# Short branch: both duals' first products ahead, weight sums on VectorE, loads on GpSimd's queue, and T4 later in the FFN front

## The chip, the core and the metric

The kernel runs on one core of one Trainium2 chip. The engines are named as the profile names them: PE is TensorE, DVE VectorE, ACT ScalarE, Pool GpSimd, and SP SyncE, which only issues transfers here. The metric is the device time of one execution in microseconds (us).

## The reference

One layer of a streaming encoder, in fp32, with 1024 positions and a width of 1024. A combined projection of the normalized input feeds two mixers and their gates; their merge goes through one more projection, and a gated FFN follows.

```python
h = rms_norm(x, norm_mix_g[l]) * (1.0 + sc1) + sh1
proj = jnp.einsum('bsd,de->bse', h, w_in[l])
b_s, c_s, v_s, v_c, gl_c, gate_br = jnp.split(proj, SPLITS[:-1], axis=-1)
y_a = b_s * causal_dwconv(c_s * v_s, conv_short_w[l])          # the short branch
y_a = jnp.einsum('bsc,cd->bsd', y_a, w_short_out[l])
u = v_c * jax.nn.sigmoid(gl_c)                                 # the conformer branch
u = causal_dwconv(u, conv_conf_w[l]) + conv_conf_b[l]
u = jax.nn.silu(layer_norm(u, conf_ln_g[l], conf_ln_b[l]))
y_b = jnp.einsum('bsc,cd->bsd', u, w_conf_out[l])
g_a, g_b = jnp.split(jax.nn.sigmoid(gate_br), 2, axis=-1)
x = x + g1 * jnp.einsum('bsd,de->bse', g_a * y_a + g_b * y_b, w_o[l])
h2 = rms_norm(x, norm_ffn_g[l]) * (1.0 + sc2) + sh2
a, bgate = jnp.split(jnp.einsum('bsd,df->bsf', h2, w_ffn_in[l]), 2, axis=-1)
x = x + g2 * jnp.einsum('bsf,fd->bsd', jax.nn.silu(a) * bgate, w_ffn_out[l])
return rms_norm(x, final_norm_g)
```

## The kernel before, in words

**Products.** Every fp32 operand is split in a high part (a cast to fp32r on ACT, `...h`) and a low part (source minus high part, on DVE or Pool, `...l`). `mm3` multiplies with three matmuls: high by high (L291), low activation by high weight (L292), high activation by low weight (L294). For weights the cast is L209 (`wh`) and the low part L210 (`wl`).

**Duals.** A pair of weight column blocks with their 1024 columns is one "dual": a 2x2 product of blocks done with seven products instead of eight, called "1", "2", "6", "5", "7", "3", "4" in this order (`PRODUCTS`). `dual_units` makes the weight operand of each. Unit "6" needs three sums of weight blocks (L233, L234, L235), unit "3" one (L237); units "1", "2" and "4" need none. `eng` says which engine sums, and by default also makes the low parts; `lo` overrides that per unit. With `early=True` each unit loads its own blocks when it is made. On the activation side the operands need differences too, such as T3 and T4 in the FFN (B22 is a plain block). The results gather in pairs of PSUM banks x, y and z; a product's result that starts a sum in another bank is copied there by ACT.

**Order.** `plan` lists the weight operands in the order of use. `next_w` takes one and lets `fetch` make those after it, so that about three are under way. Raw blocks land in `raws`, five tiles used in turn, loaded through SP's queue. The instructions of each engine are put in order by the framework's list scheduler; `tc.issue_after(ins)` makes an instruction wait its turn behind another.

**The stages that matter.** After eleven input duals come:
- the short branch, "ya": two duals, 14 products (`ya_order`, `ya_product`), on operands `tq` that `q_operands` builds. Its results are multiplied by gates `ma` that come back from HBM (`gate_dram`; L554, L557). Beside it runs the LayerNorm of the conformer branch: `ln_mean` (a matmul with ones, L732), `ln_square` per channel block, with a load of `cv`, a subtraction L743, a square and a sum L749, and `ln_rstd` (a matmul, L755).
- "yb", the conformer projection, then the join of both branches, the output projection and the second norm;
- the FFN input, 11 duals, of which the first three (`FRONT`) are interleaved with the norm: `norm_2_first`, `norm_2_half` and `norm_2_last` build the operands ("t1" for product 5, "t3" for 7, "b22" for 3, "t4" for 4). Products run in `in_order`: ... (0,"6"), (0,"5"), (0,"7"), (0,"3"), (0,"4"), (1,"6"), and so on. `in_evac` empties the banks: products 1, 6 and 5 by a copy on ACT (L980), the others by sums on DVE (L985, L989, L990) and a silu.
- hidden activations go to HBM through Pool's queue, and the FFN output follows.

Of the kernel before, what the change touches and what calls it, by code (L numbers as in the profile page):

```python
# [111 lines left out]
def block_kernel(ctx: ExitStack, tc: tile.TileContext, x0, xT, c, vecs, ada, w_first, w_plain, w_duals,  # L112
# [38 lines left out]
    def s_tile(name, dt=F32):  # L151
        return hl_tile(name, dt)
# [35 lines left out]
    def raw_tile(n=1024):  # L188

        raws.append(raws.pop(0))  # L190
        return raws[-1].tile([P, 1024], F32, tag="raw", name="raw")[:, :n]

    def load(src, n=1024):
# [21 lines left out]
    def dual_units(mats, n, early=False, eng=nc.vector, lo=None):  # L215

        a = {}

        def get(*blocks):
            for b in blocks:  # L220
                a[b] = load(mats[("11", "12", "21", "22").index(b)], n)

        def unit(m):
            if early:
                get(*{"1": ("11",), "2": ("12",), "6": ("21", "22", "11"), "3": ("12",), "4": ("22",)}.get(m, ()))
            elif m == "1":
                get("11", "12", "21", "22")
            los = (lo or {}).get(m, eng)
            if m in "12":
                return split_w(a["1" + m], n, (), los)  # L230
            if m == "6":
                a["s1"] = a["22"] if early else raw_tile(n)
                eng.tensor_tensor(a["s1"], a["21"], a["22"], ALU.add)  # L233
                eng.tensor_tensor(a["21"], a["21"], a["11"], ALU.add)  # L234
                eng.tensor_tensor(a["11"], a["11"], a["s1"], ALU.add)  # L235
            elif m == "3":
                eng.tensor_tensor(a["12"], a["12"], a["11"], ALU.add)  # L237
            return split_w(a[{"6": "11", "5": "s1", "7": "21", "3": "12", "4": "22"}[m]], n, (), los)

        return {m: (lambda m=m: unit(m)) for m in PRODUCTS}  # L240
# [4 lines left out]
    for d in range(len(PAIRS) // 2):  # L245
        units = dual_units([w_duals[d, m] for m in range(4)], 1024, eng=nc.gpsimd)
        plan += [units[m] for m in PRODUCTS]
    ya_order = [(d, m) for d in range(2) for m in "12"] + [(d, m) for d in range(2) for m in PRODUCTS[2:]]
    ya_units = [dual_units([w_short[d, m] for m in range(4)], 1024, True, nc.gpsimd, {m: nc.vector for m in "65734"})
                for d in range(2)]  # L250
    plan += [ya_units[d][m] for d, m in ya_order]
    plan += [(w[k], 1024) for w in (w_conf, w_o) for _ in range(2) for k in range(KC)]
# [76 lines left out]
    def t_split(src, hi, lo):  # L329
        nc.scalar.copy(hi, src)  # L330
        t_split.ins = nc.vector.tensor_tensor(lo, src, f32(hi), ALU.subtract).ins  # L331

    def minus(out, a, b):

        nc.vector.scalar_tensor_tensor(out=out, in0=a, scalar=-1.0, in1=b, op0=ALU.mult, op1=ALU.subtract)
# [83 lines left out]
    def uc_tile(name, n=T + CK - 1, dt=F32):  # L419
        return ucp.tile([P, T + CK - 1], dt, tag="uc", name=name)[:, :n]  # L420
# [153 lines left out]
    def q_operands(m):  # L574

        for k in range(KH):
            b11, b12, b21, b22 = (q_block(k, i) for i in range(4))
            if m == "6":
                nc.vector.tensor_tensor(b11, b11, b12, ALU.subtract)
                t2 = g_tile("t2")  # L580
                minus(t2, b11, b22)
                tq[m][k] = split(t2, hl_tile, "tq")
                minus(b21, t2, b21)
                continue
            if m == "7":
                nc.vector.tensor_tensor(b12, b22, b12, ALU.subtract)
            tq[m][k] = split({"1": b11, "2": b21, "5": b11, "7": b12, "3": b22, "4": b21}[m], hl_tile, "tq")
# [148 lines left out]

    sqs = [None, None]

    def ln_square(j):
        cv.append(uc_tile(f"cv{j}", T))  # L740
        nc.sync.dma_start(cv[j], cv_dram[j])
        for h in range(2):
            nc.vector.tensor_tensor(cv[j][:, halves[h]], cv[j][:, halves[h]], mu[h], ALU.subtract)  # L743
            sq = g_tile("sq")
            nc.scalar.activation(sq, cv[j][:, halves[h]], AF.Square, scale=1.0 / 32.0)
            if j == 0:
                sqs[h] = sq
            else:
                nc.vector.tensor_tensor(sqs[h], sqs[h], sq, ALU.add)  # L749
# [34 lines left out]
    for j in range(KC):  # L784
        conv(j)
        add_conv(j)
    ma = {}
    r0, r1, r2 = banks
    ya_banks = [{"x": r0, "y": r1, "z": r1}, {"x": r2, "y": r1, "z": r0}]
    ya_rest = {}  # L790

    def ya_product(d, m):

        w = next_w()
        bank = ya_banks[d][{"2": "y", "5": "z", "3": "z"}.get(m, "x")]
        ga = {}
        if m in "2734":
            for p in range(2):
                j, h = 2 * (2 * d + p) + (m in "74"), int(m in "73")
                ma[j, h] = ga[p] = s_tile(f"ma{j}{h}")  # L800
                nc.sync.dma_start(ga[p], gate_dram["a", j][:, halves[h]])
        for p in range(2):
            ps = bank[p]
            for k in range(KH):
                c0 = (p * KH + k) * P
                mm3([ps], slice(c0, c0 + P), w, [tq[m][k]], m in "15" and k == 0, k == KH - 1, m not in "15")
            if m == "1":
                nc.scalar.copy(ya_banks[d]["y"][p], ps)
            elif m in "65":
                ya_rest[p, m] = s_tile("v")  # L810
                nc.scalar.copy(ya_rest[p, m], ps)
            elif m == "2":
                ma["ins"] = times(ga[p], ps, ga[p]).ins
            elif m == "7":
                v = ya_rest[p, "5"]
                nc.vector.tensor_tensor(v, ps, v, ALU.add)
                ma["ins"] = minus_times(ga[p], v, ga[p]).ins
            elif m == "3":
                nc.vector.tensor_tensor(ps, ps, ya_rest[p, "6"], ALU.add)
                ma["ins"] = times(ga[p], ps, ga[p]).ins  # L820
            else:
                ma["ins"] = minus_times(ga[p], ps, ga[p]).ins

    for i, (d, m) in enumerate(ya_order):
        with ExitStack() as order:
            if i == 0:
                order.enter_context(tc.issue_after(mm3.ins))
            ya_product(d, m)
        if i in (0, 3):
            q_operands("34"[i == 3])  # L830
        elif i == 2:
            mu = ln_mean()
        elif 5 <= i < 10:
            for j in range(*((0, 2), (2, 4), (4, 6), (6, 7), (7, 8))[i - 5]):
                ln_square(j)
        elif i == 10:
            rl = ln_rstd(sqs)
        elif i == 12:
            act_b(0, 0)


    mg = [[None, None] for _ in range(KC)]

    def join(o, h, g):
# [75 lines left out]
    def norm_2_last():  # L920

        for k in range(KH):
            ts["5"][k] = t_pair("t1")
            t_split(x1[k][:, halves[0]], *ts["5"][k])
        for k in range(KH):
            b12, b22 = x1[k][:, halves[1]], x1[k + KH][:, halves[1]]
            nc.vector.tensor_tensor(b12, b22, b12, ALU.subtract)
            ts["7"][k] = t_pair("t3")
            t_split(b12, *ts["7"][k])
        for k in range(KH):  # L930
            ts["3"][k] = t_pair("b22")
            t_split(x1[k + KH][:, halves[1]], *ts["3"][k])
        b21 = [x1[k + KH][:, halves[0]] for k in range(KH)]
        for k in range(KH):
            minus(b21[k], t2[k], b21[k])
        for k in range(KH):
            ts["4"][k] = t_pair("t4")
            t_split(b21[k], *ts["4"][k])
        norm_2_last.ins = t_split.ins

    sums = {}
    for h in range(2):
# [15 lines left out]
    def in_unit(d, m):  # L958

        if d in range(1, FRONT) and m == "6":  # L960
            with tc.issue_after(norm_2_last.ins):
                return in_units[d][m]()
        return in_units[d][m]()

# [96 lines left out]
    for d, m in in_order[2 * FRONT - 1 :]:  # L1061
        if (d, m) == (FRONT - 1, "2"):
            for p in range(2):
                in_evac(d)(p, "1", in_banks[d]["x", p])
        if d in range(1, FRONT) and m == "6":
            with tc.issue_after(mm3.ins):
                in_product(d, m)
        else:
            in_product(d, m)
        if m == PRODUCTS[-1]:  # L1070
            if 2 <= d < 6:
                for i in range(40 + 2 * (d - 2), 42 + 2 * (d - 2)):
                    modulation(i, x1ap.tile([P, T], F32, tag="x1", name="ada"))
            hid_set(d)
# [211 lines left out]
```

## Time and profile before

| | us |
|---|---|
| median of 3 runs (lowest to highest) | 1493.35 (1493.24 to 1495.61) |
| the profiled execution's own time | 1494.31 |
| its span, first to last instruction | 1492.5 |
| mean granted TensorE clock | 0.996 |

| engine | busy us |
|---|---|
| PE | 1458.9 |
| DVE | 1186.0 |
| ACT | 643.6 |
| Pool | 554.4 |

A timeline row reads: start, duration, engine, line, operation, output <- input, shape, count, and in brackets the idle time ahead of it and what ended that. Rows ending in q (SPq) are an engine's queue issuing transfers. Instructions are named by line and tile; of the two versions the later one's lines are some two to twenty higher.

### The profile page before, as it was taken

Reading aid. Unit: us, or ns where it says so; the run is one execution under the profiler, and the core shown is the slowest. Engines: PE = TensorE matmul, PEld = TensorE weight load, DVE = VectorE, ACT = ScalarE, POOL = GpSimd, SP = SyncE. Lnnn points to the kernel's source line nnn. Section 1 sums busy time; section 2 is a strip of 40 time slices with the busy share of each in tenths; the row PEclk is TensorE's granted clock in tenths of the full one; section 3 lists DMA queues with packets and bytes.
Section 4 is the critical chain, followed back from the end, with each engine's and each line's share of the span. In section 5 each row is a group of like instructions: output and inputs, shape, how many; then the busy total and the mean of one; then the engine's idle time right before and its main releaser. Section 6 shows DMA issues by size and latency. Waiting matters only on the chain.

```text
span 1492.5 us, 17732 instructions
## 1 busy us (share of the span) xinstructions
PE 1458.9 (98%) x6407; PEld 1192.0 (80%) x6407; DVE 1186.0 (79%) x1615; ACT 643.6 (43%) x926; POOL 554.4 (37%) x455
## 2 busy tenths in 40 slices
PE   6999999999999998999999999999999999999997
PEld 2788888888888886778888878888888888888887
DVE  7994999989999976989687698876766665677755
ACT  4663434444433354555345464444444443222235
POOL 0027777776877676500021001100000016544005
PEclk9999999999999999999999999999999999999999
DMA  9622223223222345565585348654444449998403
GB/s 344 225 71 99 99 86 113 99 99 132 94 71 71 106 134 179 191 223 190 163 271 198 123 127 259 227 180 148 147 149 148 154 151 372 355 302 264 148 15 114
DMA packets 85882, 247.78 MB, mean 166 GB/s; under 512 B 9761, under 2 KB 11937, under 8 KB 85794
## 3 DMA queue, kind: packets, MB, share of 16 engines
q1 hardware_dynamic: 44224, 142.63, 29.0%
q0 software_dynamic: 35664, 91.24, 18.6%
q10 hardware_dynamic: 5906, 12.78, 2.2%
q8 instruction: 50, 0.82, 0.2%
q14 instruction: 38, 0.31, 0.1%
HBM read 186.31 MB, written 60.29 MB: 165 GB/s over the span
## 4 chain that ended last, share of the span: by engine, by line
PE 39%; issue 15%; POOL 3%; DVE 3%; DMA 2%; ACT 0%; POOLq 0%; DVEq 0%; ACTq 0%; SPq 0%
PE x L291 7%; PE x L292 7%; PE x L294 7%; PE z L292 3%; PE z L291 3%; PE z L294 3%; PE y L294 2%; PE y L292 2%; PE y L291 2%; DMA hid<-stage 1%; DVE cv L743 1%; DMA raw<-in_w_short 1%; PE yb L292 1%; PE yb L294 1%; PE yb L291 1%
## 5 line engine op out<-in xcount | busy, mean ns | idle before, releaser
L209 ACT CAST wh<-raw 128x1024 fp32r<-128x1024 f32 (+2 forms) x263 | 265.6, 1011 | 454.0 <-PE z L292 129.3
L210 DVE TENSOR_TENSOR wl<-raw,wh 128x1024 fp32r<-128x1024 f32 (+2 forms) x175 | 201.3, 1151 | 83.6 <-ACT wh L209 81.5
L210 POOL TENSOR_TENSOR wl<-raw,wh 128x1024 fp32r<-128x1024 f32 x88 | 219.9, 2502 | 108.4 <-ACT wh L209 108.4
L701 DVE SCALAR_TENSOR_TENSOR c<-diff,vec,c 128x512 f32<-128x512 f32 x248 | 176.5, 749 | 2.2
L1005 POOL DMA_DIRECT2D hid<-stage x71 | 37.8, 533 | 356.6 <-DVE stage L331 353.4
L292 PE MATMUL x<-tl,wh 128*128 128x512 f32 x240 | 93.4, 389 | 0.0
L294 PE MATMUL x<-th,wl 128*128 128x512 f32 x240 | 93.4, 389 | 0.0
L291 PE MATMUL x<-th,wh 128*128 128x512 f32 x240 | 93.4, 389 | 0.0
L233 POOL TENSOR_TENSOR raw<-raw 128x1024 f32<-128x1024 f32 x14 | 42.7, 3053 | 116.9 <-DVE wl L210 94.9
L701 DVE SCALAR_TENSOR_TENSOR c<-u,wsum,c 128x512 f32<-128x512 f32 x112 | 83.9, 749 | 2.0 <-ACT c L705 0.4
L291 PE MATMUL z<-th,wh 128*128 128x512 f32 x168 | 65.4, 389 | 0.0
L292 PE MATMUL z<-tl,wh 128*128 128x512 f32 x168 | 65.4, 389 | 0.0
L294 PE MATMUL z<-th,wl 128*128 128x512 f32 x168 | 65.4, 389 | 0.0
L330 ACT CAST stage<-g 128x512 fp32r<-128x512 f32 x62 | 38.3, 621 | 52.8 <-DMA hid<-stage 25.5
L331 DVE TENSOR_TENSOR stage<-g,stage 128x512 fp32r<-128x512 f32 x62 | 42.4, 686 | 19.9 <-ACT stage L330 19.8
L1031 POOL DMA_DIRECT2D th<-hid x71 | 38.1, 536 | 52.3 <-PE x L294 31.2
L272 DVE CUSTOM_DVE_ANT_0 ada<-ada,cs,vec 128x1024 f32<-128x1024 f32 x33 | 48.5, 1486 | 7.9 <-DMA ada<-in_ada 7.9
L294 PEld LDWEIGHTS x<-th,wl 128*128 128x128 f32 x240 | 45.1, 188 | 9.4
L292 PEld LDWEIGHTS x<-tl,wh 128*128 128x128 f32 x240 | 45.1, 188 | 9.3
L291 PEld LDWEIGHTS x<-th,wh 128*128 128x128 f32 x240 | 45.1, 188 | 9.3
L292 PE MATMUL y<-tl,wh 128*128 128x512 f32 x132 | 51.3, 389 | 0.0
L291 PE MATMUL y<-th,wh 128*128 128x512 f32 x132 | 51.3, 389 | 0.0
(921 smaller groups left out, 4281.7 us busy)
## 6 DMA issues: line engine op xcount, KB each, us to landing
hid<-stage POOLq DMA_DIRECT2D x71, 512.0 KB, 4.5
raw<-in_w_fi SPq DMA_DIRECT2D x53, 512.0 KB, 4.2
raw<-in_w_duals SPq DMA_DIRECT2D x48, 512.0 KB, 3.5
th<-hid POOLq DMA_DIRECT2D x71, 256.0 KB, 5.7
tl<-hid POOLq DMA_DIRECT2D x71, 256.0 KB, 5.7
ada<-in_ada SPq DMA_DIRECT2D x33, 512.0 KB, 6.2
raw<-in_w_fo SPq DMA_DIRECT2D x24, 384.0 KB, 5.8
raw<-in_w_conf SPq DMA_DIRECT2D x16, 512.0 KB, 4.2
```

Of the source, the lines that this page charges most:

```text
L209: nc.scalar.copy(wh, raw)
L210: lo = lo_engine.tensor_tensor(wl, raw, f32(wh), ALU.subtract)
L233: eng.tensor_tensor(a["s1"], a["21"], a["22"], ALU.add)
L272: nc.vector.tensor_tensor_reduce(out=raw, in0=raw, in1=cs, scale=1.0, scalar=col(V_ADA, b), op0=ALU.mult, op1=ALU.add, accum_out=modc(b),)
L291: nc.tensor.matmul(ps, wh, xh, start=first, stop=False, skip_group_check=again)
L292: nc.tensor.matmul(ps, wh, xl, start=False, stop=False, skip_group_check=again)
L294: mm3.ins = nc.tensor.matmul(ps, wl, xh, start=False, stop=last, skip_group_check=again).ins
L330: nc.scalar.copy(hi, src)
L331: t_split.ins = nc.vector.tensor_tensor(lo, src, f32(hi), ALU.subtract).ins
L701: tap.ins = nc.vector.scalar_tensor_tensor(out=out, in0=src[:, s : s + H], scalar=wt, in1=acc, op0=ALU.mult, op1=ALU.add).ins
L1005: nc.gpsimd.dma_start(hid_dram[key], s)
L1031: nc.gpsimd.dma_start(t, hid_dram[key][:, s])
```

## The change

In the short branch:
- `ya_order` runs product 1 of both duals, then product 2 of both, then the rest. Dual 1's "y" gets two banks of its own from the ps2 pool; before, both duals used `r1`.
- The eight weight sums go from Pool to DVE. Of the low parts of products 1 and 2, only that of (0,"1") stays on Pool; three more go to DVE.
- The eight loads of `cv` and the sixteen of gates go from SP's queue to Pool's. The `cv` loads are issued at the start, the gates one product ahead (`ya_gate`).
- The mean comes before the first product, the squares after products 2 to 8 (counted from 0) instead of 5 to 9, and their subtraction is ordered behind the last split; `q_operands("4")` follows product 1 instead of 3, the first `act_b` product 11 instead of 12.
- The tile `diff`, free after the convolution, is a sixth raw buffer.

In the FFN front T4's four differences and splits leave `norm_2_last` for `norm_2_t4`, emitted just before product (0,"7") and ordered behind B22's splits. Unit (0,"4") is ordered behind B22's splits, and the "6" units of duals 1 and 2 behind T4's.

```diff
     def raw_tile(n=1024):
         raws.append(raws.pop(0))
+        if raws[-1] is diffp:
+            return diffp.tile([P, T + CK - 1], F32, tag="diff", name="raw")[:, :n]
...
-    ya_order = [(d, m) for d in range(2) for m in "12"] + [(d, m) for d in range(2) for m in PRODUCTS[2:]]
-    ya_units = [dual_units([w_short[d, m] for m in range(4)], 1024, True, nc.gpsimd, {m: nc.vector for m in "65734"})
+    ya_order = [(d, m) for m in "12" for d in range(2)] + [(d, m) for d in range(2) for m in PRODUCTS[2:]]
+    ya_units = [dual_units([w_short[d, m] for m in range(4)], 1024, True, lo={"1": nc.vector if d else nc.gpsimd})
                 for d in range(2)]
...
+    def cv_load(j):
+        cv.append(uc_tile(f"cv{j}", T))
+        nc.gpsimd.dma_start(cv[j], cv_dram[j])
     def ln_square(j):
-        cv.append(uc_tile(f"cv{j}", T))
-        nc.sync.dma_start(cv[j], cv_dram[j])
         for h in range(2):
-            nc.vector.tensor_tensor(cv[j][:, halves[h]], cv[j][:, halves[h]], mu[h], ALU.subtract)
+            with tc.issue_after(split.ins):
+                nc.vector.tensor_tensor(cv[j][:, halves[h]], cv[j][:, halves[h]], mu[h], ALU.subtract)
...
+    raws.insert(0, diffp)
+    mu = ln_mean()
-    ya_banks = [{"x": r0, "y": r1, "z": r1}, {"x": r2, "y": r1, "z": r0}]
+    ya_banks = [{"x": r0, "y": r1, "z": r1}, {"x": r2, "y": [ps2_tile("y") for _ in range(2)], "z": r0}]
+    def ya_gate(d, m):
+        for p in range(2):
+            j, h = 2 * (2 * d + p) + (m in "74"), int(m in "73")
+            ma[j, h] = ya_gates[d, m, p] = s_tile(f"ma{j}{h}")
+            nc.gpsimd.dma_start(ma[j, h], gate_dram["a", j][:, halves[h]])
     def ya_product(d, m):
-        ga = {}
-        if m in "2734":
-            for p in range(2):
...
-                nc.sync.dma_start(ga[p], gate_dram["a", j][:, halves[h]])
+        ga = [ya_gates.get((d, m, p)) for p in range(2)]
...
     for i, (d, m) in enumerate(ya_order):
+        if i == 0:
+            for j in range(KC):
+                cv_load(j)
+        for e in ya_order[i + 1 : i + 2]:
+            if e[1] in "2734":
+                ya_gate(*e)
...
-        if i in (0, 3):
-            q_operands("34"[i == 3])
-        elif i == 2:
-            mu = ln_mean()
-        elif 5 <= i < 10:
-            for j in range(*((0, 2), (2, 4), (4, 6), (6, 7), (7, 8))[i - 5]):
+        if i in (0, 1):
+            q_operands("34"[i])
+        elif 2 <= i < 9:
+            for j in range(*((0, 2), (2, 3), (3, 4), (4, 5), (5, 6), (6, 7), (7, 8))[i - 2]):
                 ln_square(j)
         elif i == 10:
             rl = ln_rstd(sqs)
-        elif i == 12:
+        elif i == 11:
             act_b(0, 0)
+    raws.remove(diffp)
...
+        norm_2_last.b22 = t_split.ins
+    def norm_2_t4():
         b21 = [x1[k + KH][:, halves[0]] for k in range(KH)]
         for k in range(KH):
-            minus(b21[k], t2[k], b21[k])
+            with tc.issue_after(t_split.ins):
+                minus(b21[k], t2[k], b21[k])
...
-        norm_2_last.ins = t_split.ins
+        norm_2_t4.ins = t_split.ins
     def in_unit(d, m):
         if d in range(1, FRONT) and m == "6":
-            with tc.issue_after(norm_2_last.ins):
+            with tc.issue_after(norm_2_t4.ins):
                 return in_units[d][m]()
+        if (d, m) == (0, "4"):
+            with tc.issue_after(norm_2_last.b22):
+                return in_units[d][m]()
...
+        if (d, m) == (0, "7"):
+            norm_2_t4()
```

What that does to the engines' order shows at three places. First Pool's queue at the start of the short branch, before and then after; `wl` and `raw` are the weights' low parts and blocks, the last of the six `wl` in a row is that of (0,"1").

```order
L210 TENSOR_TENSOR wl<-raw,wh 128x1024 x6
L233 TENSOR_TENSOR raw<-raw 128x1024
L210 TENSOR_TENSOR wl<-raw,wh 128x1024
L234 TENSOR_TENSOR raw<-raw 128x1024
L210 TENSOR_TENSOR wl<-raw,wh 128x1024
L235 TENSOR_TENSOR raw<-raw 128x1024
L210 TENSOR_TENSOR wl<-raw,wh 128x1024
L237 TENSOR_TENSOR raw<-raw 128x1024
```

```order
L212 TENSOR_TENSOR wl<-raw,wh 128x1024 x6
L743 DMA cv_4481<-cv_967 128x1024
L743 DMA cv_4483<-cv_968 128x1024
L743 DMA cv_4485<-cv_969 128x1024
L743 DMA cv_4487<-cv_970 128x1024
L805 DMA ma_4545<-gate_a_107 128x512
L805 DMA ma_4547<-gate_a_109 128x512
L743 DMA cv_4489<-cv_971 128x1024
```

Pool's arithmetic ends with the `wl` of (0,"1"); what follows is loads, dual 0's first gates fifth and sixth.

Second, DVE around its first multiplications by gates (L557, then L559); `tq` are the activation operands, `y` the bank that product 2 fills. With their numbers the rows before are:

```order
L323 TENSOR_TENSOR tql_4518<-sc7_3426,tqh_4517 128x512
L210 TENSOR_TENSOR wl_4567<-raw_4561,wh_4566 128x1024
L557 TENSOR_TENSOR ma00_4527<-y_981,ma00_4527 128x512
L557 TENSOR_TENSOR ma20_4529<-y_982,ma20_4529 128x512
L323 TENSOR_TENSOR tql_4637<-sc4_2697,tqh_4636 128x512
```

and after, where wl_4552 is of (1,"2"), wl_4611 of (0,"6") and wl_4655 of (0,"5"):

```order
L239 TENSOR_TENSOR raw_4736<-raw_4736,raw_4605 128x1024
L212 TENSOR_TENSOR wl_4500<-raw_4497,wh_4499 128x1024
...
L212 TENSOR_TENSOR wl_4552<-raw_4549,wh_4551 128x1024
...
L212 TENSOR_TENSOR wl_4611<-raw_4605,wh_4610 128x1024
L325 TENSOR_TENSOR tql_4590<-sc6_3419,tqh_4589 128x512
L325 TENSOR_TENSOR tql_4594<-sc7_3426,tqh_4593 128x512
L559 TENSOR_TENSOR ma00_4545<-y_981,ma00_4545 128x512
L748 TENSOR_TENSOR cv0_4481<-cv0_4481,tot0_975 128x512
L748 TENSOR_TENSOR cv0_4481<-cv0_4481,tot1_976 128x512
L748 TENSOR_TENSOR cv1_4483<-cv1_4483,tot0_975 128x512
L559 TENSOR_TENSOR ma20_4547<-y_982,ma20_4547 128x512
L748 TENSOR_TENSOR cv1_4483<-cv1_4483,tot1_976 128x512
L212 TENSOR_TENSOR wl_4655<-raw_4603,wh_4654 128x1024
```

The sum L239 and the low parts stand on DVE ahead of the multiplications, and the squares' subtractions between them and the next low part.

Third, ACT in the FFN front, before and then after; the L980 (then L1003) copies empty bank z of product (0,"5").

```order
L330 CAST t3h<-x_6016 128x512
L209 CAST wh<-raw 128x1024
L330 CAST b22h<-x_6057 128x512
L209 CAST wh<-raw 128x1024
L330 CAST b22h<-x_6098 128x512
L330 CAST b22h<-x_6139 128x512
L330 CAST b22h<-x_6180 128x512
L330 CAST t4h<-x_6057 128x512
L330 CAST t4h<-x_6098 128x512
L330 CAST t4h<-x_6139 128x512
L330 CAST t4h<-x_6180 128x512
L980 COPY g_6915<-z 128x512
```

```order
L332 CAST t3h<-x_5936 128x512
L211 CAST wh<-raw 128x1024
L332 CAST t3h<-x_5977 128x512
L332 CAST t3h<-x_6018 128x512
L332 CAST b22h<-x_6059 128x512
L332 CAST b22h<-x_6100 128x512
L332 CAST b22h<-x_6141 128x512
L332 CAST b22h<-x_6182 128x512
L1003 COPY g_6897<-z 128x512
L1003 COPY g_6912<-z 128x512
L332 CAST t4h<-x_6059 128x512
L332 CAST t4h<-x_6100 128x512
```

The copies stand ahead of T4's casts. On DVE the sums of (1,"6") follow T4's splits in both; after the change two of bank z's operations stand among them:

```order
L331 TENSOR_TENSOR t4l<-x_6180,t4h 128x512
L985 TENSOR_TENSOR g_6915<-x,g_6915 128x512
L985 TENSOR_TENSOR g_6930<-x,g_6930 128x512
L233 TENSOR_TENSOR raw<-raw 128x1024
L234 TENSOR_TENSOR raw<-raw 128x1024
L272 ISA ada,mod<-ada,cs,vec 128x1024
L272 ISA mod 128x1
L235 TENSOR_TENSOR raw<-raw 128x1024
```

```order
L1008 TENSOR_TENSOR g_6912<-x,g_6912 128x512
L333 TENSOR_TENSOR t4l<-x_6182,t4h 128x512
L235 TENSOR_TENSOR raw<-raw 128x1024
L1012 TENSOR_TENSOR g_6861<-z,g_6861 128x512
L236 TENSOR_TENSOR raw<-raw 128x1024
L1013 TENSOR_TENSOR g_6861<-g_6861,g_6897 128x512
L237 TENSOR_TENSOR raw<-raw 128x1024
```

The last sum (L235, then L237) has moved behind L1012 and L1013, and the adaLN reduction L272 has left its place.

More of the change, by code (lines that the diff above doesn't have):

```diff
@@ L786, in block_kernel @@
         add_conv(j)
+    raws.insert(0, diffp)
     ma = {}
     r0, r1, r2 = banks
-    ya_banks = [{"x": r0, "y": r1, "z": r1}, {"x": r2, "y": r1, "z": r0}]
+    mu = ln_mean()
+    ya_banks = [{"x": r0, "y": r1, "z": r1}, {"x": r2, "y": [ps2_tile("y") for _ in range(2)], "z": r0}]
     ya_rest = {}
+    ya_gates = {}
+    def ya_gate(d, m):
[3 more added lines that the diff above has]
+            nc.gpsimd.dma_start(ma[j, h], gate_dram["a", j][:, halves[h]])
     def ya_product(d, m):
@@ L795, in ya_product @@
         bank = ya_banks[d][{"2": "y", "5": "z", "3": "z"}.get(m, "x")]
-        ga = {}
-        if m in "2734":
-            for p in range(2):
-                j, h = 2 * (2 * d + p) + (m in "74"), int(m in "73")
-                ma[j, h] = ga[p] = s_tile(f"ma{j}{h}")
-                nc.sync.dma_start(ga[p], gate_dram["a", j][:, halves[h]])
+        ga = [ya_gates.get((d, m, p)) for p in range(2)]
         for p in range(2):
```

## The prediction

> **What bounds the kernel now.** I read the page's busy shares first, then the windows to find where TensorE (PE) is not full, then PE's waits in those stretches, and then the timelines of the engines that it waits for.
>
> ```profile
> PE 1458.9 (98%) x6407; PEld 1192.0 (80%) x6407; DVE 1186.0 (79%) x1615; ACT 643.6 (43%) x926; POOL 554.4 (37%) x455
> 550.00:600.00 50.00, 44.96 (x184) 34.93 (x183) 37.37 (x43) 25.46 (x42) 28.39 (x10) 0.97 0.50 173
> 600.00:650.00 50.00, 47.47 (x203) 37.59 (x203) 46.05 (x57) 24.93 (x37) 19.98 (x6) 1.00 0.56 193
> 850.00:900.00 50.00, 46.76 (x198) 37.65 (x197) 49.97 (x72) 31.39 (x48) 0.00 (x0) 0.97 0.37 116
> ```
>
> PE is the bound: 98% of the span. So the change can only bring what PE loses at present. The windows (length, then busy time of PE, weight load, DVE, ACT, Pool, then PE's clock) show three stretches where PE is short of 50 us; the first two are the short branch, the third the front of the FFN. In the third DVE is full (49.97), in the first it is not (37.37). PE's waits from 560 to 670 (the three longest) and from 860 to 925, as total, times and longest, are:
>
> ```profile
> PE z L294 <- POOL wl L210: 3.0, 1, 3.0
> PE y L291 <- ACT y L808: 1.7, 1, 1.7
> PE x L291 <- DVE v L816: 1.3, 1, 1.3
> ...
> PE z L291 <- ACT g L980: 3.2, 1, 3.2
> PE z L294 <- DVE wl L210: 0.6, 1, 0.6
> ```
>
> **Part A, the short branch: what PE loses.** Five rows of PE's timeline give the size (start, duration): the first matmul of product 1 and the first of product 2 of dual 0, the mean, the variance, and the first matmul of the next stage, yb.
>
> ```profile
> 571.15 0.39 PE L291 MATMUL x<-tqh,wh 128*128 128x512 f32 x1
> 576.59 0.49 PE L291 MATMUL y<-tqh,wh 128*128 128x512 f32 x1
> 593.15 1.88 PE L732 MATMUL mu<-tot,ones 128*128 128x512 f32 x4
> 644.09 1.88 PE L755 MATMUL var<-sq,ones 128*128 128x512 f32 x4
> 662.17 0.39 PE L291 MATMUL yb<-zsh,wh 128*128 128x512 f32 x1
> ```
>
> A product of 24 matmuls takes 576.59 - 571.15 = 5.44 us. Fourteen products and the two sums over partitions need 14 x 5.44 + 2 x 1.88 = 79.9. The stage takes 662.17 - 571.15 = 91.0. PE loses 11.1 us, which bounds the gain of part A from above.
>
> Where it goes is one chain:
>
> ```profile
> 583.05 0.39 PE L292 MATMUL z<-tql,wh 128*128 128x512 f32 x1
> 586.40 0.57 PE L294 MATMUL z<-tqh,wl 128*128 128x512 f32 x1 [2.97 <-POOL wl L210]
> 590.39 0.40 PE L291 MATMUL z<-tqh,wh 128*128 128x512 f32 x1
> 596.72 0.50 PE L291 MATMUL y<-tqh,wh 128*128 128x512 f32 x1 [1.68 <-ACT y L808]
> 563.33 4.81 POOL L210 TENSOR_TENSOR wl<-raw,wh 128x1024 fp32r<-128x1024 f32 x1 [4.62 <-ACT wh L209]
> ...
> 581.63 2.42 POOL L234 TENSOR_TENSOR raw<-raw 128x1024 f32<-128x1024 f32 x1 [3.99 <-DMA raw<-in_w_short]
> 586.37 5.01 SPq L195 DMA_DIRECT2D raw<-in_w_short  x2
> 591.48 1.80 SPq L801 DMA_DIRECT2D ma<-gate_a  x4
> 595.31 1.41 DVE L557 TENSOR_TENSOR ma<-y,ma 128x512 f32<-128x512 f32 x2 [3.20 <-DMA ma<-gate_a]
> 596.09 0.57 ACT L808 COPY y<-z 128x512 f32<-128x512 f32 x1 [5.81 <-DVE ma L557]
> ```
>
> Pool's sum L234 stands ahead of the low part (wl) of dual 1's product 1, and waits 3.99 us for a block; so PE waits 2.97 us for that wl. The ten matmuls after it take 590.39 - 586.40 = 3.99 us where ten at the usual spacing, 5.44 / 24 = 0.227, take 2.27: a slow clock of 0.97 in that window, 1.7 us more. Meanwhile SP holds the gate loads behind two weight loads that wait for Pool's wl; the gates are issued at 591.48, DVE multiplies at 595.31, and only then may ACT copy dual 1's start (its product 1 stands in the banks that the profile calls z) into bank y, which both duals share. That is PE's second wait. The waits after 620 have another cause:
>
> ```profile
> 599.22 1.23 DVE L210 TENSOR_TENSOR wl<-raw,wh 128x1024 fp32r<-128x1024 f32 x1
> 611.20 10.54 POOL L233 TENSOR_TENSOR raw<-raw 128x1024 f32<-128x1024 f32 x1 [16.87 <-DVE sq L749]
> 573.09 6.31 DVE L323 TENSOR_TENSOR tql<-q,tqh 128x512 fp32r<-128x512 f32 x4 [1.33 <-ACT tqh L322]
> 579.32 2.49 DVE L323 TENSOR_TENSOR tql<-sc,tqh 128x512 fp32r<-128x512 f32 x4
> 589.79 2.32 DVE L210 TENSOR_TENSOR wl<-raw,wh 128x1024 fp32r<-128x1024 f32 x1 [7.98 <-ACT wh L209]
> 622.22 2.88 DVE L554 SCALAR_TENSOR_TENSOR ma<-v,ma 128x512 f32<-128x512 f32 x1
> ```
>
> Beside Pool's sums, DVE and Pool slow each other: four tql splits take 6.31 us beside Pool and 2.49 alone, one wl 2.32 against 1.23, a product L554 2.88, and a Pool sum 10.54 where L234 above takes 2.42.
>
> **What the change takes and adds there.** Dual 1's banks of its own remove the wait of ACT for DVE's multiply. The sums and three low parts leave Pool, so the 3.99 us block on Pool and the slow pairs go. They are added to DVE: 8 sums and 3 wl, 11 x 1.23 = 13.5 us, of which successive ones overlap a little. DVE has that: its idle time in the chain was 1.33 + 7.98 + 3.20 = 12.5 us, and the slow rows just quoted alone give back (6.31 - 2.49) + (2.32 - 1.23) = 4.9, with more in the second set of sums. What DVE has in front of PE decides: PE's n-th product would start at 571.15 + 1.88 + 5.44 x (n - 1). Adding up the rows' durations along DVE's new order (an estimate), the wl of the second product is done at about 572 against PE's 579, that of (0,"6"), the fifth, at 587 against 595, of (0,"5") at 593 against 600, of (1,"6"), the tenth, at 616 against 622. It stays 6 to 8 us ahead, so I take the whole 11.1, with half of it as the lower bound.
>
> The loads move to Pool's queue. They are 24 issues (8 of cv, 16 of gates), and Pool has one row of arithmetic left in this stage. The nearest issue from Pool is that of the gates for branch b:
>
> ```profile
> L856 POOL DMA_DIRECT2D gb<-gate_b x16: 536/536/722, 645.4 to 746.2; - x16
> ```
>
> Each takes 0.54 us of Pool at the median, 0.72 at most, among DVE work. 24 x 0.54 = 13 us over 80 us, and six issues before dual 0's first gate are 3.2 us: hidden. SP loses the same 24 issues, so its weight loads no longer stand behind cv and gates. The diff tile as a sixth raw buffer only lets loads start sooner. The mean ahead of the first product and squares sooner move work; they cost PE the same 1.88 us each. The extra issue_after on the subtractions holds DVE's squares behind the split; what is behind them in DVE's queue is the next wl, which has the 6 to 8 us.
>
> **Part B, the FFN front.** PE reaches product 3 of dual 0 at 882.71, one spacing after 882.48:
>
> ```profile
> 882.48 0.39 PE L294 MATMUL x<-t3h,wl 128*128 128x512 f32 x1
> 886.11 0.50 PE L291 MATMUL z<-b22h,wh 128*128 128x512 f32 x1 [3.24 <-ACT g L980]
> 893.33 0.39 PE L291 MATMUL x<-t4h,wh 128*128 128x512 f32 x1
> 879.41 1.05 ACT L209 CAST wh<-raw 128x1024 fp32r<-128x1024 f32 x1 [3.77 <-DVE raw L237]
> 883.40 2.17 ACT L330 CAST t4h<-x 128x512 fp32r<-128x512 f32 x4
> 885.48 1.05 ACT L980 COPY g<-z 128x512 f32<-128x512 f32 x2
> 892.39 1.22 DVE L235 TENSOR_TENSOR raw<-raw 128x1024 f32<-128x1024 f32 x1
> 893.52 0.68 DVE L989 TENSOR_TENSOR g<-z,g 128x512 f32<-128x512 f32 x1
> 893.70 2.00 ACT L209 CAST wh<-raw 128x1024 fp32r<-128x1024 f32 x2 [4.16 <-DVE raw L235]
> ```
>
> The copies that free bank z (885.48) stand behind four t4h casts on ACT (2.17), and those behind wh, which waited 3.77 us for a sum of DVE. So product 4 starts at 893.33 instead of 882.71 + 5.44 = 888.15: 5.2 us lost, its slow clock included (again 0.97). In the new order the copies stand ahead of t4h and T4's four differences leave DVE's queue in front of that sum (4 x 0.6 = 2.4 us, as t4l's spacing, 2.49 for four in the tql row of the same shape). ACT's copies end at about 882.5, so the 5.2 us go.
>
> What is late next: T4's differences and splits now stand on DVE ahead of the sums of (1,"6"), with the second wait as before: L235 ended 893.6, and the new order puts two more half-width operations (1.2 us) in front of the last sum and moves one adaLN reduction of about that size behind it. I put the last sum's end at 893.6 to 894.8, its wh 1 us later. PE, no longer held, wants (1,"6") at 888.15 + 5.44 = 893.6, and waits 2.1 us for the high part and 0.4 for the low. The later wait of 0.6 for a wl loses about 0.5 of itself. Part B is 5.2 - 2.5 + 0.5 = 3.2; bounds 0 (the new wait eats all) and 5.7.
>
> The new wait's clock is one place for a rule. In this trace a wait of 1.68 us was not followed by slow matmuls, waits of 2.97 and 3.24 were. A wait of 2.1 lies nearer to the first, so I take no slow clock; the other end is 1.7 us more. [...]
>
> **The sum.** 11.1 + 3.2 = 14.3 us. The profiled execution took 1494.31 (span 1492.5), the median of three runs is 1493.35; the gain is taken from the profiled spans, so 1493.35 - 14.3 = 1479.0, and 1480.0 for an execution like the profiled one. About 0.2%, 3.0 us, is what a measurement here can tell from no change.
>
> **Rivals.**
> 1. *The new wait eats part B.* DVE is full in 850 to 900, so anything added ahead of (1,"6")'s sums is paid one for one. With a wait of 3 us and 1.7 of slow clock part B falls to about 0.5, 1482. For: 49.97 of 50 busy. Against: the work ahead of the last sum hardly grows. Chance 0.15.
> 2. *No new wait in the FFN.* If the sums come in time, 5.7 instead of 3.2: 1476.5. Chance 0.10.
> 3. *DVE becomes the bound of the short branch.* 13.5 us are added to a stage in which DVE was busy 46.05 of 50 us from 600 to 650. If half of part A returns as waits for wl, the time is 1484.6. For: the second window. Against: the slow pairs there (2.88 for 0.68) are Pool's doing and go with its sums. Chance 0.18.
> 4. *The gain is given back later*, where PE waits for nothing now but DVE is busy too (yb and join): 1490 to 1493. Chance 0.04.
> 5. *Slower: Pool's queue as the bound.* Pool issues in order, and dual 0's first gates stand fifth and sixth. DVE multiplies by them ahead of the wl of (0,"5"), so late gates stop PE. If an issue beside DVE's work took as long as the sum at 611.20 was stretched, 10.54 - 2.42 = 8 us, six issues from 568 (the end of Pool's wl of 563.33, which stays) would end at 616, land some 5 us later, and with 3 us more to that wl PE, which wants it at 600, would wait 24 us: 1479.0 + 24 = 1503. It turns to a loss from about 6.4 us an issue ((14.3 + 600 - 568 - 8) / 6). Against it: 0.54 in the row of gb. Chance 0.08. [...]
>
> **Chances and range.** The forecast holds 0.45, with its own range of 1477.5 to 1481.5. Cases 1 to 3 and the forecast together are 0.88 and all faster; case 4 is the no change, 0.04; case 5 slower, 0.08. The range of 8 in 10 runs from case 2 less 1.5 of term errors, 1475.0, to just over case 3, 1486.0.
>
> **What would show it.** PE's first matmul of yb should come 79 to 81 us after the mean's start; its waits for POOL wl, ACT y and DVE v should be gone, and no Pool arithmetic of 10 us be left. DVE's 128x512 operations should read 0.68 throughout the stage. In the FFN, ACT g ahead of product 3 should be gone, and a wait of about 2 us for ACT wh stand at (1,"6") in its place. A stage over 86 us with waits for DVE wl would be rival 3; long idle of DVE ahead of L559 for ma would be rival 5.

## The result and the profile after

| | us |
|---|---|
| before, median of 5 runs (lowest to highest) | 1493.25 (1493.04 to 1495.61) |
| after, median of 5 runs | 1482.34 (1480.81 to 1487.19) |
| ratio after / before, 95% interval | 0.9929, 0.9909 to 0.9949 |
| the profiled execution after, and its span | 1482.34, 1480.6 |

The change makes the kernel 0.7% faster, 10.9 us by the medians. The forecast was 1479.0 with a range of 1475.0 to 1486.0; the time lies inside that range, but outside the forecast's own band of 1477.5 to 1481.5. After's runs spread over 6 us, before's over 2.6.

The same rows as before, from the page and the windows (length, then busy PE, weight load, DVE, ACT, Pool, then PE's clock, the DMA engines' share and GB/s):

```profile
PE 1454.6 (98%) x6407; PEld 1189.3 (80%) x6407; DVE 1184.1 (80%) x1626; ACT 641.8 (43%) x926; POOL 528.1 (36%) x468
550.00:600.00 50.00, 50.00 (x219) 40.70 (x218) 44.77 (x56) 28.99 (x48) 17.38 (x21) 1.00 0.61 223
600.00:650.00 50.00, 48.99 (x211) 39.02 (x210) 45.31 (x64) 24.02 (x34) 5.34 (x10) 1.00 0.54 182
850.00:900.00 50.00, 48.26 (x210) 38.63 (x209) 47.33 (x67) 30.63 (x47) 2.13 (x5) 1.00 0.43 136
```

From 550 to 600 PE is full (44.96 before) and its clock is 1.00 where it was 0.97. From 850 to 900 PE is busy 48.26 (46.76 before), and its clock is 1.00 there too. PE's waits from 560 to 670, then from 850 to 920:

```profile
PE yb L294 <- DVE zsl L325: 1.2, 1, 1.2
PE z L293 <- DVE v L826: 0.7, 1, 0.7
PE x L293 <- DVE v L826: 0.3, 1, 0.3
...
PE x L293 <- ACT wh L211: 1.7, 1, 1.7
```

The waits for Pool's low part and for ACT's y are gone. Of the waits for DVE's v 0.3 and 0.7 are left, and two new waits stand there, one in yb (1.2) and one in the FFN front (1.7). The stage's ends, then the second's start in the FFN front, from PE's timeline:

```profile
570.77 1.88 PE L734 MATMUL mu<-tot,ones 128*128 128x512 f32 x4
652.20 0.39 PE L293 MATMUL yb<-zsh,wh 128*128 128x512 f32 x1
653.77 0.50 PE L294 MATMUL yb<-zsl,wh 128*128 128x512 f32 x1 [1.18 <-DVE zsl L325]
874.89 0.39 PE L293 MATMUL z<-b22h,wh 128*128 128x512 f32 x1
887.66 0.50 PE L293 MATMUL x<-t2h,wh 128*128 128x512 f32 x1 [1.68 <-ACT wh L211]
```

The stage took 652.20 - 570.77 = 81.4 us, 9.6 less than before's 91.0. Following the two traces' starts of the same matmuls, the gain is 10.0 us at yb (0.4 stood before the stage began), 8.4 at the mix, 7.8 before product (0,"3"), 12.2 once the front is over, and 11.9 at the end (the spans: 1492.5 - 1480.6).

Where part A fell short shows on DVE. Its waits from 570 to 655 after, and the landing times of the `cv` loads and of the gates (lowest, median, highest):

```profile
DVE ma L559 <- DMA ma<-gate_a: 5.0, 2, 3.0
DVE raw L274 <- DMA raw<-in_ada: 4.7, 1, 4.7
DVE raw L239 <- DMA raw<-in_w_short: 0.2, 1, 0.2
...
DMA to landing us min/median/max: 5.4/9.0/9.9
...
DMA to landing us min/median/max: 2.9/7.2/10.1
```

Before, `cv` landed in 5.5 us and the gates in 5.0 (medians). Pool's queue shows when the loads are asked for:

```profile
580.04 2.31 POOL L743 DMA_DIRECT2D cv<-cv  x4 [14.62 <-DVE tql L325]
582.34 1.07 POOL L805 DMA_DIRECT2D ma<-gate_a  x2
```

The first `cv` load waits 14.6 us, until DVE's splits have read the tile that it is to fill, and dual 0's first gates stand behind four `cv` loads. From there eight loads of 512 KB and the first gates are asked for within ten microseconds; from 580 to 600 the DMA engines are busy 0.99 of the time (0.69 before), and the first two gates land 9.2 and 9.6 us after they were asked for. DVE stands still 5.0 us for gates, with the wl of (0,"5") behind it, and later 4.7 for an adaLN block that stands in its order ahead of the variance's reciprocal root. That used up most of the 6 to 8 us that DVE was ahead. The low part of (1,"6"), and PE's first use of it:

```profile
620.28 1.22 DVE L212 TENSOR_TENSOR wl<-raw,wh 128x1024 fp32r<-128x1024 f32 x1
622.54 0.39 PE L296 MATMUL z<-tqh,wl 128*128 128x512 f32 x1
```

It is done at 621.5, where the estimate was 616; 1 us was left.

### The profile page after: what moved, and what is told of

It is laid out like the page before. It is cut to its first block, busy times and chain, and to the rows that moved or that the text cites. A ratio compares the mean times of both kernels' runs of the same rounds, so it can differ in the third digit from the quotient of the medians.

```text
span 1480.6 us, 17737 instructions
## 1 busy us (share of the span) xinstructions
PE 1454.6 (98%) x6407; PEld 1189.3 (80%) x6407; DVE 1184.1 (80%) x1626; ACT 641.8 (43%) x926; POOL 528.1 (36%) x468
## 4 chain that ended last, share of the span: by engine, by line
PE 86%; DVE 6%; issue 3%; DMA 2%; POOL 2%; ACT 0%; POOLq 0%; ACTq 0%; DVEq 0%
PE x L293 10%; PE x L294 10%; PE x L296 10%; PE z L294 7%; PE z L296 7%; PE z L293 7%; PE y L296 6%; PE y L294 6%; PE y L293 6%; PE yb L294 2%; PE mix L293 2%; PE yb L296 2%; PE mix L294 2%; PE mix L296 2%; PE yb L293 2%
## 5 line engine op out<-in xcount | busy, mean ns | idle before, releaser
L212 POOL TENSOR_TENSOR wl<-raw,wh 128x1024 fp32r<-128x1024 f32 x85 | 209.7, 2471 | 108.4 <-ACT wh L211 108.4
L212 DVE TENSOR_TENSOR wl<-raw,wh 128x1024 fp32r<-128x1024 f32 (+2 forms) x178 | 204.4, 1149 | 49.5 <-ACT wh L211 47.9
L235 POOL TENSOR_TENSOR raw<-raw 128x1024 f32<-128x1024 f32 x12 | 29.8, 2483 | 95.3 <-DVE wl L212 94.5
```

The costliest lines, as they stand in the source:

```text
L212: lo = lo_engine.tensor_tensor(wl, raw, f32(wh), ALU.subtract)
```

## The experiments

Each kernel ran beside the kernel before on the same chip; times are medians.

| kernel | us | before beside it | difference |
|---|---|---|---|
| after, second time | 1482.93 | 1493.66 | -10.7 |
| short branch alone | 1483.61 | 1493.28 | -9.7 |
| FFN alone | 1490.25 | 1493.28 | -3.0 |
| sums and low parts on DVE, alone | 1488.17 | 1493.04 | -4.9 |
| order, banks, mean first, alone | 1497.47 | 1493.66 | +3.8 |
| after, sums back on Pool | 1498.67 | 1493.28 | +5.4 |
| after, sums on Pool and loads on SP | 1498.64 | 1493.66 | +5.0 |
| after, no diff tile | 1485.49 | 1493.04 | -7.6 |
| after, cv loads spread | 1479.76 | 1493.66 | -13.9 |
| after, loads on SP | 1480.11 | 1493.28 | -13.2 |
| loads on SP, sums first in the FFN | 1479.66 | 1493.04 | -13.4 |
| the same, cv loads spread | 1478.97 | 1493.04 | -14.1 |

**Each part alone.** The first keeps all but the FFN's edits, the second has only those. Of the first's edit, the last lines:

```diff
...
-        if (d, m) == (0, "7"):
-            norm_2_t4()
...
```

> The short branch's edits without the FFN's. In the trace of the changed kernel the gain over the kernel before stands at 10.0 us when yb starts (0.4 of it from before the short branch), at 8.4 when the mix starts and at 7.8 in the FFN front. My theory: the two parts are independent, so this kernel keeps 8 us: 1485, with PE's wait of about 3.2 us for ACT's copies of g in the FFN front as before, its slow clock included. Rival: an FFN front that is reached earlier finds its operands no readier, or a later stage gives the gain back; then the time is above 1489. Rival: nearly all comes from here and the FFN edit only moves a wait: below 1483.

> The kernel before with only the FFN's edits (T4 behind B22). My theory: 4 to 4.5 us, 1489, as the gain grew from 7.8 to 12.2 us over the FFN front in the changed kernel's trace; a wait of about 1.7 us for ACT wh at (1,"6") without slow matmuls. Rival: the wait there is longer than 2.97 us or brings the slow clock, and the part gives under 2 us: above 1491.

1483.61 (ratio 0.9939, 0.9926 to 0.9951) and 1490.25 (0.9979, 0.9970 to 0.9988). They add up to 12.7 against 10.7 to 10.9 together, within their spread; the FFN alone brought less than the 4 to 4.5 I expected. In the first, PE waits for nothing in the stage and 0.6 us for zsl. Its stage takes 650.52 - 570.84 = 79.7 us, 1.7 less than in the profile of after, though the code of the short branch is the same. Its clock is 0.97 again from 850 to 900, with the old wait:

```profile
PE z L293 <- ACT g L995: 3.2, 1, 3.2
```

In the second that wait is gone, the clock there is 1.00, and PE waits 1.7 us for ACT's wh at (1,"6"), as in after.

**The sums back on Pool, with the loads on Pool or on SP.**

```diff
-    ... dual_units([w_short[d, m] for m in range(4)], 1024, True, lo={"1": nc.vector if d else nc.gpsimd})
+    ... dual_units([w_short[d, m] for m in range(4)], 1024, True, nc.gpsimd, {m: nc.vector for m in "65734"})
```

> The changed kernel with the eight weight sums and the three low parts back on Pool. My theory: Pool's in-order sums are the cause of most of part A; PE waits for POOL wl or for sums again, DVE's operations beside Pool read 1.5 to 3 us instead of 0.69, and the time rises by 5 to 10 us, 1487 to 1492; as Pool also issues the loads, gates behind a sum come later still. Rival: the order and the banks did it, and DVE or Pool for the sums is the same: within 2 us of the changed kernel.

> The changed kernel with both undone: sums and three low parts on Pool, cv and gate loads on SP's queue. With the sums alone back on Pool the time was 1498.7, and its trace shows DVE's eight tql splits at 13.31 us beside Pool. My theory: that is contention of DVE with Pool, not loads stuck behind sums, so 1494 to 1499 here too. Rival: Pool's in-order queue with loads behind sums was the cost, and the loads on SP bring it back to 1485 or less.

1498.67 (1.0041, 1.0028 to 1.0053) and 1498.64 (1.0032, 1.0020 to 1.0045): slower than before, the first by more than I expected, and the loads' queue makes no difference. So it isn't loads stuck behind sums. With the sums and loads on Pool: DVE's timeline, a wait of PE, and a later sum of Pool; below them the like row of DVE after:

```profile
582.60 13.31 DVE L325 TENSOR_TENSOR tql<-sc,tqh 128x512 fp32r<-128x512 f32 x8
...
615.60 0.79 PE L296 MATMUL x<-tqh,wl 128*128 128x512 f32 x1 [4.12 <-DVE wl L212]
...
620.25 8.87 POOL L239 TENSOR_TENSOR raw<-raw 128x1024 f32<-128x1024 f32 x1 [4.75 <-DMA raw<-in_w_short]
```

```profile
583.78 2.50 DVE L325 TENSOR_TENSOR tql<-sc,tqh 128x512 fp32r<-128x512 f32 x4
```

Eight splits take 13.31 us beside Pool and 2 x 2.50 = 5.0 without it. They are not all slow: one of the eight, started at 583.20, takes 9.10 us while Pool makes two low parts and a sum (583.51 to 591.74), and the last four, with only loads on Pool, take 2.48 together. DVE is busy all of 550 to 600 (50.00), and the wl for which PE waits 4.12 us takes DVE 3.36 us (612.19) beside a sum of Pool. So a split that takes 0.6 us where Pool only issues loads (2.48 / 4 = 0.62) took 9.10 beside Pool's arithmetic.

**Order and banks alone, and sums alone.**

> The kernel before with only the order of the products (1s, then 2s), dual 1's own banks and the mean at the start; sums, low parts, loads, raw buffers and FFN as before. My theory: PE's waits for ACT y (1.7) goes, but Pool's sums still stand ahead of low parts and slow DVE, so PE's wait for POOL wl stays about 3 us with its slow clock, and the time is 1490 to 1494. Rival: the order is what matters, and 5 us or more come from it alone: under 1488.

> The kernel before with only the eight sums and three low parts moved from Pool to DVE; order, banks, loads, raw buffers, squares and FFN as before. The changed kernel without this one edit is at 1498.7, and order and banks without it at 1497.5, so it must carry the short branch's gain. My theory: the waits for POOL wl, the slow clock and the slow DVE operations go; what is left is ACT y behind the gates, as both duals share a bank: 1484 to 1488. Rival: it needs the new order and banks too, and alone gives under 3 us, above 1490.

Order, banks and mean on the kernel before cost 3.8 us (1497.47, ratio 1.0027, 1.0017 to 1.0038). Both of my readings missed: I had expected 1490 to 1494, the rival under 1488. PE's longest waits there:

```profile
PE y L294 <- POOL wl L210: 4.7, 1, 4.7
PE x L291 <- DVE v L817: 4.3, 1, 4.3
```

Pool makes wl of (0,"2") only after three sums, so the wait of 3.0 has become 4.7. The wait of 4.3 is for DVE, which takes 5.47 us for two sums of squares (621.31) and 3.35 for a low part (626.71) beside Pool's sums. The clock is 0.93 in both windows of the stage. The sums alone bring 4.9 (1488.17, 0.9966, 0.9952 to 0.9979), a little less than I expected. What is left in the stage is one wait, with a slow clock behind it (0.97 from 550 to 600):

```profile
PE y L291 <- ACT y L808: 2.9, 1, 2.9
```

That is the wait which the new order and the second pair of banks remove. The order needs the sums moved: it costs 3.8 without that, while both, with the other short-branch edits, give 9.7. No run has these two alone together.

**The loads' queue, and the loads spread.** Loads back on SP's queue at the same places; or on Pool's queue, two `cv` loads at the start and one per product from the third on. Between them the kernel of after ran again.

```diff
-        nc.gpsimd.dma_start(cv[j], cv_dram[j])
+        nc.sync.dma_start(cv[j], cv_dram[j])
...
-            nc.gpsimd.dma_start(ma[j, h], gate_dram["a", j][:, halves[h]])
+            nc.sync.dma_start(ma[j, h], gate_dram["a", j][:, halves[h]])
```

```diff
-            for j in range(KC):
+            for j in range(2):
                 cv_load(j)
+        if 2 <= i < 8:
+            cv_load(i)
```

> The changed kernel with the cv and gate loads issued at the same places but on SP's queue again. My theory: what held the gates before was SP waiting for Pool's low parts, and those waits went with the sums; so the queue matters little, within 2 us of the changed kernel (1481 to 1484), and DVE still idles 2 to 5 us for gates because the same 6 MB are asked for at once. Rival: the move of the queue is what freed the weight loads; then SP's queue holds weight loads behind cv loads that wait for DVE, PE waits for wh or wl in the short branch again, and the time rises by 4 us or more, above 1486.

> The changed kernel unaltered, beside the next three on one chip, as their yardstick and to see its spread. Its first five runs went from 1480.8 to 1487.2, those with the loads on SP's queue from 1478.8 to 1482.8. My theory: the spread comes from when the gates land, since DVE waits 4.4 to 5.0 us for them, and this run's profile shows that wait again; 1481 to 1484. Rival: the spread comes from somewhere else (a wait of PE's that names no releaser stood in the FFN output of two of the profiles), and DVE's wait for gates here is under 2 us in a run of the same time.

> The changed kernel with the cv loads on Pool's queue spread out: two at the start, then one per product from the third on, instead of eight at once. My theory: the eight at once fill the DMA engines (8 x 512 KB landed in 9.0 us each instead of 5.5) and the gates behind them land late; spread, cv lands in about 5.5 us, DVE's wait for gates falls from 5 us to under 2, and PE's waits for v and zsl (0.3 + 0.7 + 1.2) mostly go: 1479 to 1481. Rival: gates come as late by Pool's queue whatever stands ahead of them, and the time stays within 1 us of the changed kernel; or the squares come late now and var is waited for: above 1484.

After's second time is 1482.93 (0.9926, 0.9912 to 0.9939), its runs from 1479.2 to 1485.0, and DVE waits 5.0 us for gates again. With SP it is 1480.11 (0.9909, 0.9893 to 0.9924), spread it is 1479.76 (0.9911, 0.9899 to 0.9924). The intervals overlap after's; that each is 2 to 3 us faster is likely, not shown by itself. The profiles show more. On SP, DVE's waits and the issues with their median landing:

```profile
DVE ma L556 <- DMA ma<-gate_a: 1.7, 1, 1.7
DVE ma L559 <- DMA ma<-gate_a: 0.3, 1, 0.3
...
cv<-cv SPq DMA_DIRECT2D x8, 512.0 KB, 6.6
ma<-gate_a SPq DMA_DIRECT2D x16, 256.0 KB, 4.8
```

```profile
571.35 1.45 PE L734 MATMUL mu<-tot,ones 128*128 128x512 f32 x3
651.03 0.39 PE L293 MATMUL yb<-zsh,wh 128*128 128x512 f32 x1
```

The stage takes 651.03 - 571.35 = 79.7 us there, what 14 products and the two sums need; PE waits for nothing up to 670. So the move to Pool's queue isn't what frees PE: in these profiles it costs a little. The first gates are asked for at about the same time (581.78 on SP, 582.34 on Pool) and the DMA engines are as full from 580 to 600 (0.96 and 0.99), but gates land in 4.8 instead of 7.2 us, and L559's waits for gates are 0.3 us instead of 5.0.

Spread on Pool's queue, `cv` still landed in 8.8 and the gates in 7.0, not in the 5.5 I expected. But the edit hardly spread the loads: they were asked for from 579.7 to 590.6, where after has 580.0 to 588.9, as Pool runs ahead of the products. So it does not decide whether the crowd on the DMA engines makes them late. What it moved is dual 1's first gates: they stand ahead of the last two `cv` loads and are asked for at 586.73 instead of 589.43 and 591.30. DVE waited 3.1 us for gates instead of 5.0, the second of the two waits being gone, and PE's waits up to 670 were gone too.

The spread of after's runs has other sources than the gates: its two profiled executions have the same 5.0 us, at 1482.34 and 1481.27. One profile on SP has a wait of 1.7 us in the FFN output that names no releaser. The rest is open.

**The diff tile.**

> The changed kernel without the diff tile as sixth raw buffer. My theory: it is not needed for PE, as DVE waits only 0.2 us for a weight block; but in the changed kernel DVE waits 3.5 to 4.7 us for an adaLN block (raw<-in_ada) ahead of rstd, and a shorter rotation moves those loads: within 2 us of the changed kernel, 1480 to 1485. Rival: with five buffers DVE waits for weight blocks in its sums, PE for wl, and the time is 1486 or more.

1485.49 (0.9946, 0.9934 to 0.9959), just above what I expected and 2.6 to 3.1 above after; the intervals overlap, so the tile is likely, not surely, worth that. With five buffers DVE's waits for blocks are

```profile
DVE raw L235 <- issue: 2.8, 1, 2.8
DVE raw L236 <- DMA raw<-in_w_short: 2.6, 1, 2.6
DVE raw L239 <- DMA raw<-in_w_short: 2.3, 1, 2.3
```

where after has 0.2, and PE waits 4.7 us in all from 560 to 670, where after has 2.2. This is the cost of sums in DVE's queue: DVE waits for the loads that Pool used to wait for (3.99 us before). This kernel also shows what the spread kernel couldn't. DVE's later splits spread its `cv` loads on Pool's queue over 577.3 to 595.8 (18.5 us instead of 8.9), the DMA engines are busy 0.78 from 580 to 600 (0.99 in after), and `cv` lands in 4.9 us (median) instead of 9.0. So here the loads that were asked for further apart landed sooner. Whether the queue counts by itself is not separated: on SP the 24 loads share it with the weight blocks, eight of w_short in that trace.

**The wait at (1,"6"), and the best version.** On the kernel with the loads on SP, bank z's two sums behind the last weight sum; then with the `cv` loads spread as well.

```diff
...
+                with ExitStack() as order:
+                    if d == 0:
+                        order.enter_context(tc.issue_after(dual_units.ins))
-                nc.vector.tensor_tensor(t, ps, t, ALU.add)
+                    nc.vector.tensor_tensor(t, ps, t, ALU.add)
```

> The changed kernel with the loads on SP's queue (1480.1 in five rounds), and in the FFN front bank z's two sums of dual 0 ordered behind the last weight sum of (1,"6"). My theory: PE's wait of 1.7 us for ACT wh is set by DVE's order; two operations of 0.6 us less ahead of the sum take it to 0.5 us: 1.2 us less, 1479.0, which only the profile can tell. Rival: the wait is ACT's or bank z's, stays 1.7 or moves to the next product.

> The kernel of the run before this one with the cv loads spread as well (two at the start, then one per product). A trial of the best version. My theory: spread brought about 3 us on Pool's queue where DVE waited 5 us for gates; on SP it waits 0.3 + 1.7 us, so there is at most 1 us left: 1478 to 1480. Rival: the spread loads stand in SP's queue ahead of weight blocks and wait for DVE to free their tiles, so PE waits for wl: above 1482.

1479.66 and 1478.97 (0.9911, 0.9898 to 0.9925; 0.9907, 0.9894 to 0.9921). PE's wait stayed, 1.6: my theory fell. DVE's last sum, ACT and PE in the first:

```profile
882.01 1.22 DVE L237 TENSOR_TENSOR raw<-raw 128x1024 f32<-128x1024 f32 x1
...
883.20 0.60 ACT L1019 ACTIVATE g<-x 128x512 f32<-128x512 f32 x1
883.69 2.94 ACT L211 CAST wh<-raw 128x1024 fp32r<-128x1024 f32 x3
...
884.78 0.50 PE L293 MATMUL x<-t2h,wh 128*128 128x512 f32 x1 [1.62 <-ACT wh L211]
```

The sum ends at 883.23, but ACT first runs the silu of product 4's second half, which can't start before PE is through with that product (its last matmul starts at 882.77, the silu at 883.20); wh follows. In after the sum (886.53) and that silu ended together, so both held wh. With wh ahead of the silu as well the wait would be some 0.5 us shorter (883.69 - 883.23), an estimate; it wasn't tried. The last kernel has the best median of all, 1479.0, and no wait of PE up to 670; it can't be told from the other three with eased loads.

## Why the prediction came out as it did

- **Part A's mechanism was right.** The waits for Pool's low part and for y are gone, the slow clock with them, and DVE's operations read 0.69. The runs add that neither the sums nor the order does it alone: -4.9 and +3.8. Two of its signs missed: yb came after 81.4 us, not 79 to 81, and waits for DVE's v were left.
- **Part A's size, 11.1, was 9.6, and 1.6 of that went in yb** (10.0 to 8.4). The step that failed is the loads, "24 issues at 0.54 us, hidden". The issues took 0.53 to 0.54 (median) as said. Two terms were left out. One is when the first can be issued: at 580.04, not at 568, because its tile was still being read. The other is when the loads land: with the DMA engines at 0.99 and on Pool's queue the gates took 2.2 us longer than before, the first ones over 4 us longer, and DVE waited. With the loads on SP the stage took 79.7, the full 11.1 (91.0 - 79.7 = 11.3). The loss isn't constant: the same code took 81.4 and 80.4 us in the two executions of after, and 79.7 in that of the short branch alone.
- **The lead of 6 to 8 us** that was to cover this held for wl, but only by 1 us at (1,"6"), which is luck. It didn't hold for what DVE does last: v (0.3 + 0.7) and zsl (1.2). The walk through DVE's order had no waits for DMAs in it: 5.0 us for gates, 4.7 for the adaLN block. Which of these two costs PE how much was not run apart.
- **Part B: 3.2 forecast, 4.4 in the trace** (7.8 to 12.2), 3.0 by the medians of the FFN alone. A wait of about 2 us for wh at (1,"6") came, at 1.7 us, and no 0.4 for the low part followed. No slow clock followed it either (1.00 from 850 to 900, the next matmuls 0.39 to 0.50 us), but that leaves the choice for 2.1 us untested. Its cause was only half right: DVE's sums and ACT's silu end together.
- **The rivals.** Rival 3 (DVE as the bound) is what remained of part A, at a fifth of its price. Rival 4 happened as to its place, yb, with 1.6 us. Rival 5 had the right place, gates behind `cv` on Pool's queue ahead of the wl of (0,"5"), and the wrong price: no issue was stretched (0.72 at most for `cv`). What held the queue was the tile, and the late landing cost 5 us of DVE, not 24 of PE.
- **The sum** was 14.3. By the spans it was 11.9: 0.4 from before the stage, 9.6 for part A, less 1.6 in yb and 0.6 up to product (0,"3"), 4.4 for part B, less 0.3 to the end. By the medians it was 10.9, because the profiled execution of before was 1.1 us above its median. Part B's surplus of 1.2 hides a part of what part A and yb lack, and that is luck as well. Eased loads bring 13.2 to 14.1.

## What to carry to other kernels

Before counting an engine's idle time as room for moved work, walk its new order with the DMA waits in it: with the sums DVE took over waits for their blocks, 2.6 and 2.3 us with five raw buffers, 0.2 with six, and it stood 5.0 us for gates. Ask also when the tile of a load that is moved forward comes free: the first `cv` load stood 14.6 us in Pool's queue until its tile had been read, and the first gates, behind four such loads, were issued only at 582.34; so what is multiplied first should be asked for first. Where a step seems to give nothing or to cost, try it beside the step that removes its partner: the order of the products cost 3.8 us while Pool still made the sums.

## What the runs showed of the hardware

The traces show which waits of PE were followed by a slow clock. Six waits of 1.62 to 1.73 us (one each before, after, with the loads on SP, without the diff tile and in the last two kernels) were followed by no slow matmuls, only by ones of 0.39 to 0.50 us. Five of 2.94 to 3.24 us (before 2.97 and 3.24, sums alone 2.94 and 3.24, short branch alone 3.23) all were, by six or seven matmuls of 0.63 us each. In the kernel with sums and loads on Pool two waits in between were followed by slow ones; a third there, of 1.82, ran into the next wait after two matmuls:

```profile
671.79 0.50 PE L293 MATMUL yb<-zsh,wh 128*128 128x512 f32 x1 [1.86 <-DVE ma L556]
672.13 0.50 PE L294 MATMUL yb<-zsl,wh 128*128 128x512 f32 x1
672.42 0.63 PE L296 MATMUL yb<-zsh,wl 128*128 128x512 f32 x1
...
1292.20 0.47 PE L293 MATMUL z<-th,wh 128*128 128x512 f32 x1 [2.20 <-issue]
...
1293.43 0.56 PE L296 MATMUL z<-th,wl 128*128 128x512 f32 x1
1293.78 0.63 PE L293 MATMUL z<-th,wh 128*128 128x512 f32 x1
```

So a wait of 2.1 us, which the forecast took as safe, need not be, and in the second of these the slow matmuls began 1.23 us after PE had resumed (1293.43 - 1292.20). The first of the two stands 5.4 us behind another wait, of 1.25. But the length of a wait alone does not decide it. With sums on Pool and loads on SP a wait of 3.43 us was followed by no slow matmul at all:

```profile
588.73 0.50 PE L296 MATMUL y<-tqh,wl 128*128 128x512 f32 x1 [3.43 <-POOL wl L212]
589.07 0.40 PE L293 MATMUL y<-tqh,wh 128*128 128x512 f32 x1
590.02 0.39 PE L294 MATMUL y<-tql,wh 128*128 128x512 f32 x1
```

What decides in the range from 1.86 to 3.43 us is open here.
